# Two-layer trunk on one core: start addresses of the matmul operands in SBUF, modulo 256 bytes

## The chip, the cores and the metric

The kernel runs on one core of one Trainium2 chip. A core has a matrix engine (PE; its weight loads are listed apart as PEld), a vector engine (DVE), a scalar engine (ACT), a general engine (POOL) and a queue engine that issues DMAs (SP). SBUF is the on-chip memory that feeds the engines: 128 partitions, each a line of bytes; a tile takes the same byte range in every partition. PSUM receives the matmuls' results. The metric is the device time of one execution in microseconds; faster, same and slower are called at 2%.

## The reference

The input is x of shape (1, 256, 2048) in float32. Two layers follow, each a mixer and a squared-ReLU feed-forward, with RMS norms around both:

```python
for layer in range(2):
    y = rmsnorm(h, norm_w[layer, 0])
    if layer % 2 == 0:
        y = linear_attention_mixer(y, ...)   # gated DeltaNet heads | retention heads, one projection in, one out
    else:
        y = spatial_gating_mixer(y, ...)     # gelu(h @ w_in) -> u, v;  (u * (tril(W_s) layernorm(v) + b)) @ w_out
    h = h + rmsnorm(y, norm_w[layer, 1])
    y = squared_relu_mlp(rmsnorm(h, norm_w[layer, 2]), ffn_w_up[layer], ffn_w_down[layer])
    h = h + rmsnorm(y, norm_w[layer, 3])
```

`squared_relu_mlp` is `square(relu(h @ w_up)) @ w_down` with w_up (2048, 8192) and w_down (8192, 2048). The weights are read once each from HBM, some 475 MB in all, so the kernel is a stream of weights against 256 rows of activations.

## The kernel before

**Products in three matmuls.** A float32 product is made of matmuls in a reduced type. Each operand is split in a high part and a low remainder, and three matmuls per product are summed in PSUM: high x high, low x high, high x low. For weights, `weights` (lines 121 to 133) takes a block of 128 x 2048, loads it into `raw`, lets ACT write `whi` (line 131) and DVE write `wlo` (line 132). Activations are split the same way by `split` (lines 193 to 199).

**Which operand moves.** A matmul holds one operand of 128 x 128 in the array (it is loaded first, by a weight load, PEld) and streams the other, the moving one, past it. There are three kinds of loops:
- `prod_tok` (lines 135 to 140), called by `chunk_tok`, `first_chunk` and `down_last`: the activations, 128 rows of tokens, are held, and the weights move, up to 512 columns. It does all large products of the mixers, and in the feed-forward the first chunk of the up projection, column block 3 and half of column block 1 of the down projection, and its last block of rows.
- `up_pass` (lines 313 to 328): the weights are held, 128 columns of them, and the activations move, 256 tokens. It makes chunks 1 to 15 of the up projection.
- `chunk7` (lines 355 to 389): seven products instead of eight of a 2 x 2 block product, from sums of activations (`f`) and sums of weights (`qsum`); activations are held, 256 columns of weights move. It makes the rest of the down projection.

While one matmul runs, the next one's operand is loaded. The order in which blocks follow each other is written out in the feed-forward (`ORDER`, `FIRST`), and in the mixers small tasks are put between blocks by a counter (`spawn`, `tick`).

**Where tiles lie.** Pools of tiles are laid one behind the other from byte 1152 of a partition (below that are a scratch area and constants), and within a pool tiles lie in the order in which they are first asked for. The order of the pools is `gap`, `wp`, `cp`, `xp`, `hp`, and above them the pool of the stage at work: `l0`, `ffn1`, `sg`, `ffn3`.
- `gap` holds one unused tile of `PAD0` = 896 bytes (line 110), so `wp` begins at 2048. `wp` has 3 `raw`, 4 `whi` and 4 `wlo` of 8192 bytes, all at 0 modulo 256.
- `cp` holds small tiles, with an unused one of `PAD1` = 544 bytes in front (line 111), so that `xp` begins at 97280, again 0.
- `xp` holds the normed activations, `xh0` to `xh3` and `xl0` to `xl3` of 4096 bytes: all at 0. `new_x` makes them three times over: in layer 0's mixer (line 498) and in `down_last` (line 258) for the stage that follows.
- `hp` and the stage pools begin at 0 too. In the feed-forward, `e0`, `e1` (activations of the down projection) and `f0`, `f1` (their sums), each a pair of high and low tiles of 4096 bytes made by `pair` (line 387), lie at 0. In `sg`, two small tiles of 192 bytes come first, so that `v0` to `v7` lie at 128 and, after four more small ones, `u` and `e0` to `e3` at 0.
- `sg` uses its tiles twice: the gated activations that `sg_out` multiplies lie by turns in `e0` to `e3` (at 0) and in `v0` to `v7` (at 128). In layer 0 the held operand of the output projection lies in tiles of `hp` and `l0`, at 0 but for `Um0` and `Um1`, at 224.

Slices keep the place: a block of 512 weight columns is 2048 bytes, one of 256 is 1024, 128 tokens are 512 bytes. Only the first projection differs: it takes 400 columns of a block at a time, 1600 bytes, so that its four slices lie at 0, 64, 128 and 192.

Of the kernel before, what the change touches and what calls it, by code (L numbers as in the profile page):

```python
# [10 lines left out]
F32 = mybir.dt.float32  # L11
F32R = mybir.dt.float32r
# [5 lines left out]
P = 128  # L18
D = 2048
SEQ = 256  # L20
# [9 lines left out]
PARTS = [4, 2, 1, 1]  # L30
WAIT = [26, 30]
AHEAD = 200
PAD0, PAD1 = 896, 544
WARM = 10
SEVEN, KEPT = (0, 1, 2), 1
ORDER = (None, 0, None, 1, None, 2, None, 3)
# [59 lines left out]
def program(tc, nc, A, S):  # L96
# [3 lines left out]
    xp = tc.alloc_tile_pool(name="xp", bufs=1)  # L100
# [5 lines left out]
    V, G, ACT, PE, DMA = nc.vector, nc.gpsimd, nc.scalar, nc.tensor, nc.sync  # L106
    uid = [0]
    ahead = [0]

    V.memset(gap.tile([P, PAD0 // 4], F32, tag="gap0", name="gap0"), 0.0)  # L110
    V.memset(cp.tile([P, PAD1 // 4], F32, tag="gap1", name="gap1"), 0.0)

    def T(pool, shape, tag, dt=F32, bufs=None):
        uid[0] += 1
        kw = {} if bufs is None else {"bufs": bufs}
        return pool.tile(shape, dt, tag=tag, name=f"{tag}_{uid[0]}", **kw)
# [81 lines left out]
            ACT.activation(hi, src, AF.Copy, scale=col)  # L198
            V.scalar_tensor_tensor(lo, src, col, hi.bitcast(F32), ALU.mult, ALU.subtract)

    def group(pool, th, tl, bufs=None):
        return T(pool, [P, 4, SEQ], th, F32R, bufs), T(pool, [P, 4, SEQ], tl, F32R, bufs)

    def kts(groups):
        return [(e[0][:, j, :], e[1][:, j, :]) for e in groups for j in range(4)]

    def new_x(n=4):
        return [group(xp, f"xh{g}", f"xl{g}") for g in range(n)]

    def to_channels(src, dst, b, col=None):  # L210
        tp = bank(tpp, 512, "tp")
# [28 lines left out]
    h = [[None] * 4 for _ in range(2)]  # L240
# [14 lines left out]

    def down_last(s, X, rows, w1, w0, yw, rpend):
        units = [weights(s, [(r, [(c * 512, 512)]) for r in rows]) for c in range(4)]
        newx = None if w0 is None else new_x()
        rh = [None, None]
        rv = [None, None]  # L260
        for b in range(2):
            ssy = small(4, "ssy")
            yb = yw(b)
            for c in range(4):
                ps = bank(acc, 512, "acc")
                for j in range(4):
                    prod_tok(ps, X[j], b, units[c], j, 512, j == 0, j == 3)
                yt = y[b][c]
                V.tensor_tensor(yt, ps, yt, ALU.add)  # L269
                square_sum(ssy[:, c : c + 1], yt)  # L270
                (V if c == 3 else G).tensor_tensor(yb[c], yt, w1[c], ALU.mult)  # L271
                if c == 2:
                    base = small(1, "base")
                    V.tensor_reduce(base, ssy[:, 0:3], AX.X, ALU.add)
                    V.tensor_scalar(base, base, 1.0 / D, EPS if rpend is None else rpend[b], ALU.mult, ALU.add)
            rs = small(1, "rs")
            V.tensor_scalar(rs, ssy[:, 3:4], 1.0 / D, base, ALU.mult, ALU.add)
            rsqrt(rs, rs)
            for c in range(4):
                ht = h[b][c]  # L280
                V.scalar_tensor_tensor(ht, yb[c], rs, ht, ALU.mult, ALU.add)  # L281
                if w0 is None:
                    DMA.dma_start(A["out"][b * P : (b + 1) * P, c * 512 : (c + 1) * 512], ht)
                else:
                    (V if c == 0 else G).tensor_tensor(yb[c], ht, w0[c], ALU.mult)
                    to_channels(yb[c], newx[c], b)
        if w0 is not None:
            for b in range(2):
                ssh = small(4, "ssh")
                for c in range(4):  # L290
                    square_sum(ssh[:, c : c + 1], h[b][c])
                rh[b] = T(cp, [P, 1], f"rh{b}", bufs=2)
                tot = small(1, "tot")
                V.tensor_reduce(tot, ssh, AX.X, ALU.add)
                var = small(1, "var")
                V.tensor_scalar(var, tot, 1.0 / D, EPS, ALU.mult, ALU.add)
                rsqrt(rh[b], var)
                rv[b] = T(cp, [P, 1], f"rv{b}", bufs=2)
                V.tensor_scalar(rv[b], var, var, EPS, ALU.mult, ALU.mult)
            newx = kts(newx)  # L300
        return newx, rh, rv
# [81 lines left out]
    def ffn(up, dn, X, rh, w1i, w0i):  # L383
        last = HID // 512 - 1
        with tc.tile_pool(name=f"ffn{w1i}", bufs=1, reuse_waits="tile") as fp:

            def pair(name):
                return T(fp, [P, 4, SEQ], f"{name}h", F32R), T(fp, [P, 4, SEQ], f"{name}l", F32R)

            def relu2(ps):  # L390
                r = T(fp, [P, 512], "rl", bufs=3)
# [65 lines left out]
            t = []  # L457
# [36 lines left out]
    def layer0_mixer():  # L494
        rstd = [T(cp, [P, 1], f"rh{b}", bufs=2) for b in range(2)]
        s = S["la_in"]
        with tc.tile_pool(name="l0", bufs=1, reuse_waits="tile") as lp:
            xg = new_x()
            X = kts(xg)
            spans0 = [(4096, 16), (3072, 384)]  # L500
            ps = [bank(acc, 400, "acc") for _ in range(2)]
# [512 lines left out]
    def layer1_mixer(X, rh):  # L1014
        si, so = S["sg_in"], S["sg_out"]
        with tc.tile_pool(name="sg", bufs=1, reuse_waits="tile") as gp:
            ws = T(gp, [P, 8, P], "ws")
            DMA.dma_start(ws, A["ws"].rearrange("p (g t) -> p g t", t=P))
            G.affine_select(ws, ws, pattern=[[0, 8], [1, P]], compare_op=ALU.is_ge, fill=0.0, base=0,
                            channel_multiplier=-1)  # L1020
            v = [None] * 8
            st = [T(gp, [P, 8, 6], f"st{b}") for b in range(2)]

            def v_evac(c, b, ps):
                if v[c] is None:
                    v[c] = T(gp, [P, 2, 512], f"v{c}")
                ACT.activation(v[c][:, b, :], ps, AF.Gelu_apprx_tanh, scale=rh[b])
                V.bn_stats(st[b][:, c, :], v[c][:, b, :])

            for b, ps in first_chunk(si, X, [(SGW, 512)]):  # L1030
                v_evac(0, b, ps)
            for c in range(1, 8):
                ps = chunk_tok(si, X, ALLK, [(SGW + c * 512, 512)], 512)
                for b in range(2):
                    v_evac(c, b, ps[b])
            rs, mu = [], []
            for b in range(2):
                mv = T(gp, [P, 2], f"mv{b}")
                V.bn_aggr(mv, st[b])
                var = small(1, "var")  # L1040
                V.tensor_scalar(var, mv[:, 1:2], EPS, None, ALU.add)
                r = T(gp, [P, 1], f"lr{b}")
                rsqrt(r, var)
                rs.append(r)
                mu.append(mv[:, 0:1])

            tags = ["e0", "e1", "e2", "e3", "v0", "v1", "v2", "v3", "e0", "e1", "e2", "e3", "v4", "v5", "v6", "v7"]
            gts = [None] * 8

            def gate(g):  # L1050
                wb = T(hp, [P, 512], "bc", bufs=4)
                DMA.dma_start(wb, A["lnw"][:, g * 512 : (g + 1) * 512].partition_broadcast(P))
                bb = T(hp, [P, 512], "bc", bufs=4)
                DMA.dma_start(bb, A["lnb"][:, g * 512 : (g + 1) * 512].partition_broadcast(P))
                pss = []
                for b in range(2):
                    t = v[g][:, b, :]
                    V.tensor_scalar(t, t, mu[b], rs[b], ALU.subtract, ALU.mult)
                    G.tensor_tensor(t, t, wb, ALU.mult)
                    G.tensor_tensor(t, t, bb, ALU.add)  # L1060
                ps = chunk_tok(si, X, ALLK, [(g * 512, 512)], 512)
                us = []
                for b in range(2):
                    pm = bank(mxp, 512, "mx")
                    PE.matmul(pm, ws[:, g, :], v[g][:, b, :], start=True, stop=True)  # L1065
                    u = T(gp, [P, 512], "u", bufs=2)
                    ACT.activation(u, ps[b], AF.Gelu_apprx_tanh, scale=rh[b])
                    V.scalar_tensor_tensor(u, pm, bsc[:, g : g + 1], u, ALU.add, ALU.mult)
                    us.append(u)
                dst = (T(gp, [P, 4, SEQ], tags[2 * g], F32R), T(gp, [P, 4, SEQ], tags[2 * g + 1], F32R))  # L1070
                for b in range(2):
                    blocks_split(T(hp, [P, 512], "bc", bufs=4), us[b], dst, b)
                gts[g] = kts([dst])

            def rows(g):
                return [g * 512 + j * P for j in range(4)]

            gate(0)
            for a in (0, 2, 4):
                gate(a + 1)  # L1080
                gate(a + 2)
                down(so, gts[a] + gts[a + 1], rows(a) + rows(a + 1), a == 0)
            gate(7)
            down(so, gts[6], rows(6), False)

            def rows_in(tags):
                t = [T(gp, [P, 2, 512], g) for g in tags]
                return [t[0][:, 0], t[0][:, 1], t[1][:, 0], t[1][:, 1]]

            w1 = row_load(rows_in(["v0", "v1"]), "nrow", 2)  # L1090
            w0 = row_load(rows_in(["v2", "v3"]), "nrow", 6)
            return down_last(so, gts[7], rows(7), w1, w0, lambda b: rows_in(["e0", "e1"]), None)
# [62 lines left out]
```

## Time and profile before

| | us |
|---|---|
| median of 2 runs | 2518.86 (2517.79 to 2519.94) |
| profiled execution | 2520.84, span of its instructions 2519.1 |
| layer 0, mixer | from 0 to about 540 |
| layer 0, feed-forward | about 540 to 1255 |
| layer 1, mixer | about 1255 to 1803 |
| layer 1, feed-forward | about 1803 to 2519 |

The profile names an instruction by engine, source line and tiles, out<-in with buffer numbers left out; in a matmul's name the moving operand stands first, the held one second (`acc<-whi,xh`: weights move past activations; `tp<-xh,whi`: activations move past weights). A group's row has its count, the busy time and mean duration of one, and the idle time before it. Matmuls overlap in the pipeline and their ends are modelled, so the share of busy time of PE says that it always had a matmul under way, not how fast they followed each other; that is read from the distance of two starts. A row of the windows view has the window, its length, then the busy time and number of instructions of each engine, the granted clock of PE, the share of the DMA engines and GB/s.

### The profile page before, as it was taken

To read this page: it belongs to the slowest core of one execution; us is meant where nothing else is said; L and a number is where in the kernel's file an instruction comes from. 1 tells how busy PE (TensorE), PEld (TensorE's weight loads), DVE (VectorE), ACT (ScalarE), POOL (GpSimd) and SP (SyncE) were. 2 spreads that over 40 slices of the span, in tenths; PEclk is the share of its full clock that TensorE was granted. 3 is DMA by queue.
4 is the path that set the end of the run, shared out by engine and by line. 5 is a ranking of instruction groups with operands and counts; after the bars stand their busy time and mean duration, and the time that the engine had idled before them with its cause. 6 is when DMAs were issued, how large, how long until landed. Compare 5 with 4: busy or idle time off the path is not lost.

```text
span 2519.1 us, 37114 instructions
## 1 busy us (share of the span) xinstructions
PE 2485.1 (99%) x15418; PEld 2234.5 (89%) x15418; DVE 1984.7 (79%) x2322; ACT 1260.5 (50%) x1266; POOL 183.2 (7%) x144
## 2 busy tenths in 40 slices
PE   9999999999999999999999999999999999999998
PEld 8788888879999999999878878888799999999997
DVE  6586855578898889889864596876888988988897
ACT  6655444455455545455554434333555545555553
POOL 0001201130000000000210110110300000000001
PEclk9999999999999999999999999999999999999999
DMA  8444544644554555555455455555445555555553
GB/s 310 164 154 152 191 157 175 213 159 184 204 190 180 197 200 193 192 202 203 182 218 188 181 208 209 196 197 200 151 185 202 189 194 201 201 184 184 201 203 132
DMA packets 81832, 480.17 MB, mean 191 GB/s; under 512 B 13696, under 2 KB 15872, under 8 KB 27392
## 3 DMA queue, kind: packets, MB, share of 16 engines
q1 hardware_dynamic: 81664, 477.80, 52.5%
q8 instruction: 121, 1.98, 0.3%
q14 instruction: 47, 0.39, 0.0%
HBM read 475.14 MB, written 2.62 MB: 190 GB/s over the span
## 4 chain that ended last, share of the span: by engine, by line
PE 46%; DVE 3%; POOL 1%; issue 0%; ACT 0%; DVEq 0%; POOLq 0%; ACTq 0%
PE acc L138 8%; PE acc L140 8%; PE acc L139 8%; PE tp L326 5%; PE tp L325 5%; PE tp L324 5%; PE acc L368 1%; PE acc L370 1%; PE acc L369 1%; PE mx L370 1%; PE mx L369 1%; PE mx L368 1%; DVE h L281 1%; DVE wlo L132 1%; PE mx L1065 1%
## 5 line engine op out<-in xcount | busy, mean ns | idle before, releaser
L132 DVE TENSOR_TENSOR wlo<-raw,whi 128x2048 fp32r<-128x2048 f32 (+3 forms) x366 | 824.8, 2256 | 264.4 <-ACT whi L131 254.9
L131 ACT ACTIVATE whi<-raw 128x2048 fp32r<-128x2048 f32 (+3 forms) x366 | 686.4, 1876 | 469.9 <-PE acc L139 286.8
L326 PE MATMUL tp<-xh,wlo 128*128 128x256 f32 x1920 | 543.5, 283 | 0.0
L325 PE MATMUL tp<-xl,whi 128*128 128x256 f32 x1920 | 543.3, 283 | 0.0
L324 PE MATMUL tp<-xh,whi 128*128 128x256 f32 x1920 | 543.1, 283 | 0.0
L138 PE MATMUL acc<-whi,xh 128*128 128x512 f32 (+3 forms) x1120 | 439.3, 392 | 3.2 <-ACT whi L131 3.2
L140 PE MATMUL acc<-wlo,xh 128*128 128x512 f32 (+3 forms) x1120 | 431.5, 386 | 1.8 <-DVE wlo L132 0.9
L139 PE MATMUL acc<-whi,xl 128*128 128x512 f32 (+3 forms) x1120 | 431.8, 385 | 0.0
L324 PEld LDWEIGHTS tp<-xh,whi 128*128 128x128 f32 x1920 | 368.4, 192 | 1.7
L325 PEld LDWEIGHTS tp<-xl,whi 128*128 128x128 f32 x1920 | 368.4, 192 | 1.7
L326 PEld LDWEIGHTS tp<-xh,wlo 128*128 128x128 f32 x1920 | 368.4, 192 | 0.0
L138 PEld LDWEIGHTS acc<-whi,xh 128*128 128x128 f32 x1120 | 211.2, 189 | 43.5 <-ACT whi L131 4.4
L140 PEld LDWEIGHTS acc<-wlo,xh 128*128 128x128 f32 x1120 | 210.7, 188 | 42.9 <-DVE wlo L132 2.9
L195 ACT ACTIVATE whi<-qsum 128x2048 fp32r<-128x2048 f32 x74 | 141.7, 1915 | 210.4 <-DVE qsum L349 166.7
L139 PEld LDWEIGHTS acc<-whi,xl 128*128 128x128 f32 x1120 | 211.3, 189 | 38.7 <-issue 1.0
L196 DVE TENSOR_TENSOR wlo<-qsum,whi 128x2048 fp32r<-128x2048 f32 x74 | 169.4, 2290 | 66.1 <-ACT whi L195 66.1
L195 ACT ACTIVATE whi<-raw 128x1536 fp32r<-128x1536 f32 x74 | 110.2, 1489 | 184.5 <-DMA raw<-dn 70.2
L431 DVE TENSOR_TENSOR y<-acc,y 128x512 f32<-128x512 f32 x136 | 92.3, 686 | 56.0 <-PE acc L370 54.8
L196 DVE TENSOR_TENSOR wlo<-raw,whi 128x1536 fp32r<-128x1536 f32 x74 | 129.6, 1751 | 2.4 <-ACT whi L195 2.3
L271 POOL TENSOR_TENSOR e0h<-y,f1h 128x512 f32<-128x512 f32 x8 | 13.0, 1648 | 1364.8 <-DVE y L269 1364.8
L138 PE MATMUL acc<-whi,e0h 128*128 128x512 f32 x256 | 100.0, 391 | 0.0
L139 PE MATMUL acc<-whi,e0l 128*128 128x512 f32 x256 | 100.0, 391 | 0.0
(357 smaller groups left out, 4347.6 us busy)
## 6 DMA issues: line engine op xcount, KB each, us to landing
raw<-up SPq DMA_DIRECT2D x128, 1024.0 KB, 4.8
raw<-dn SPq DMA_DIRECT2D x128, 1024.0 KB, 4.8
raw<-sg_in SPq DMA_DIRECT2D x64, 1024.0 KB, 4.8
raw<-la_in SPq DMA_DIRECT2D x56, 1024.0 KB, 4.8
raw<-sg_out SPq DMA_DIRECT2D x32, 1024.0 KB, 4.8
raw<-la_out SPq DMA_DIRECT2D x16, 1024.0 KB, 4.7
raw<-la_in SPq DMA_DIRECT2D x4, 768.0 KB, 8.2
kq<-xT SPq DMA_DIRECT2D x8, 256.0 KB, 6.3
```

The costliest lines, as they stand in the source:

```text
L131: ACT.activation(a, r, AF.Copy)
L132: V.tensor_tensor(d, r, a.bitcast(F32), ALU.subtract)
L138: PE.matmul(ps, xh, wh, start=first, stop=False)
L139: PE.matmul(ps, xl, wh, start=False, stop=False)
L140: PE.matmul(ps, xh, wl, start=False, stop=last)
L195: ACT.activation(hi, src, AF.Copy)
L196: V.tensor_tensor(lo, src, hi.bitcast(F32), ALU.subtract)
L324: PE.matmul(out, wh[:, col], xh, start=k == 0 and m % 2 == 0, stop=False, skip_group_check=True)
L325: PE.matmul(out, wh[:, col], xl, start=False, stop=False, skip_group_check=True)
L326: PE.matmul(out, wl[:, col], xh, start=False, stop=k == NKT - 1, skip_group_check=True)
L368: PE.matmul(ps, x[k][0], wh, start=k == 0, stop=False, skip_group_check=True)
L431: V.tensor_tensor(Y[k, c], p, Y[k, c], ALU.add)
```

## The change

The paddings become 192 and 224 bytes. `wp` then begins at 1152 + 192 = 1344, which is 64 modulo 256: all weights, split or not, lie at 64. `cp` shifts with it, and `xp` begins at 96256, again 0, so `hp` and the stage pools still begin at 0.

The tiles of `xp` are made larger, 4160 and 4288 bytes, and hold the activations at an offset: `X_IN` = (64, 0) or `X_UP` = (0, 192), bytes within the high and the low tile. A low tile begins at 64 modulo 256, so `X_IN` puts both parts at 64 and `X_UP` both at 0. `down_last` takes `X_UP` where a mixer ends (there `rpend` is `None` and a feed-forward follows) and `X_IN` where a feed-forward ends.

`skip` makes an unused tile and writes zeros into it on POOL. In the feed-forward, 128 bytes of it stand before and behind each pair of `e0`, `f0`, `e1`, `f1` when it is first asked for: the pairs lie at 128, the other tiles of that pool at 0 as before. In `sg`, 192 bytes behind the two first small tiles put `v0` to `v7` at 64, and 128 bytes later put `u` and `e0` to `e3` at 64.

| operands of a matmul (held, moving), bytes modulo 256 | before | after |
|---|---|---|
| up projection, chunks 1 to 15 (weights, activations) | 0, 0 | 64, 0 |
| up projection, first chunk (activations, weights) | 0, 0 | 0, 64 |
| down projection (e or f, weights) | 0, 0 | 128, 64 |
| layer 0 input, layer 1 input (activations, weights) | 0, 0 | 64, 64 |
| layer 1 output, from e (activations, weights) | 0, 0 | 64, 64 |
| layer 1 output, from v (activations, weights) | 128, 0 | 64, 64 |
| layer 0 output (activations, weights) | 0 (Um 224), 0 | 0 (Um 224), 64 |

No instruction is taken away and none is moved; 18 memsets are added, and the two gap memsets become shorter.

```diff
-PAD0, PAD1 = 896, 544
+PAD0, PAD1 = 192, 224
+X_IN, X_UP = (64, 0), (0, 192)
...
+    def skip(pool, n):
+        uid[0] += 1
+        G.memset(pool.tile([P, n // 4], F32, tag=f"skip{uid[0]}", name=f"skip{uid[0]}"), 0.0)
...
-    def group(pool, th, tl, bufs=None):
-        return T(pool, [P, 4, SEQ], th, F32R, bufs), T(pool, [P, 4, SEQ], tl, F32R, bufs)
+    def group(g, at):
+        t = T(xp, [P, 1040], f"xh{g}", F32R), T(xp, [P, 1072], f"xl{g}", F32R)
+        return [a[:, o // 4 : o // 4 + 1024].rearrange("p (j t) -> p j t", t=SEQ) for a, o in zip(t, at)]
...
-    def new_x(n=4):
-        return [group(xp, f"xh{g}", f"xl{g}") for g in range(n)]
+    def new_x(at):
+        return [group(g, at) for g in range(4)]
...
-        newx = None if w0 is None else new_x()
+        newx = None if w0 is None else new_x(X_UP if rpend is None else X_IN)
...
             def pair(name):
-                return T(fp, [P, 4, SEQ], f"{name}h", F32R), T(fp, [P, 4, SEQ], f"{name}l", F32R)
+                if name in seen:
+                    return T(fp, [P, 4, SEQ], f"{name}h", F32R), T(fp, [P, 4, SEQ], f"{name}l", F32R)
+                seen.add(name)
+                skip(fp, 128)
+                hi = T(fp, [P, 4, SEQ], f"{name}h", F32R)
+                lo = T(fp, [P, 4, SEQ], f"{name}l", F32R)
+                skip(fp, 128)
+                return hi, lo
+
+            seen = set()
...
-            xg = new_x()
+            xg = new_x(X_IN)
...
             st = [T(gp, [P, 8, 6], f"st{b}") for b in range(2)]
+            skip(gp, 192)
...
+            skip(gp, 128)
             tags = ["e0", "e1", "e2", "e3", "v0", "v1", "v2", "v3", "e0", "e1", "e2", "e3", "v4", "v5", "v6", "v7"]
```

## The prediction

> **What bounds the kernel now.** I read the page's busy shares first, then the same by slice, then who waited for whom on PE, then the two feed-forward stretches alone.
>
> ```profile
> span 2519.1 us, 37114 instructions
> ...
> PE 2485.1 (99%) x15418; PEld 2234.5 (89%) x15418; DVE 1984.7 (79%) x2322; ACT 1260.5 (50%) x1266; POOL 183.2 (7%) x144
> ...
> PE   9999999999999999999999999999999999999998
> ...
> PEclk9999999999999999999999999999999999999999
> ```
>
> ```profile
> PE mx L697 <- DVE PT L700: 4.2, 3, 2.3
> ```
>
> ```profile
> 600.00:1235.00 635.00, 632.73 (x4762) 609.69 (x4761) 559.73 (x550) 333.47 (x255) 0.00 (x0) 1.00 0.54 194
> 1850.00:2510.00 660.00, 659.47 (x4938) 634.05 (x4937) 580.78 (x578) 343.70 (x272) 7.90 (x7) 1.00 0.52 189
> ```
>
> The matrix engine is busy in every slice, its granted clock is full, and its longest wait (4.2 us in all) is small. The two windows (length, then PE, PEld, DVE, ACT, POOL) lie within the two feed-forward layers: PE has no gap, DVE is at 559.73/635 = 88%. So the time is the pace at which matmuls follow each other, and a change of places pays or costs only through that pace. It must be read from start to start, because a matmul's end is modelled:
>
> ```profile
> 763.66 0.39 PE L140 MATMUL acc<-wlo,e0h 128*128 128x512 f32 x1
> ...
> 764.57 0.28 PE L324 MATMUL tp<-xh,whi 128*128 128x256 f32 x1
> 764.68 0.28 PE L325 MATMUL tp<-xl,whi 128*128 128x256 f32 x1
> 764.80 0.28 PE L326 MATMUL tp<-xh,wlo 128*128 128x256 f32 x1
> ...
> 765.88 0.28 PE L326 MATMUL tp<-xh,wlo 128*128 128x256 f32 x1
> ```
>
> Four 512-column matmuls take 764.57 - 763.66 = 0.91 us, 227 ns each; nine 256-column ones take 765.88 - 764.80 = 1.08 us, 120 ns each. The recorded durations keep a fixed distance to the pace (283 and 120, 391 and 227: about 163 ns), so a difference of durations in a grouped view is a difference of pace. The groups by form, with their counts:
>
> ```profile
> L326 PE MATMUL tp<-xh,wlo 128*128 128x256 f32 x1920 | 543.5, 283 | 0.0
> L325 PE MATMUL tp<-xl,whi 128*128 128x256 f32 x1920 | 543.3, 283 | 0.0
> L324 PE MATMUL tp<-xh,whi 128*128 128x256 f32 x1920 | 543.1, 283 | 0.0
> ...
> L138 PE MATMUL acc<-whi,e0h 128*128 128x512 f32 x256 | 100.0, 391 | 0.0
> ...
> L140 PE MATMUL acc<-wlo,v 128*128 128x512 f32 x128 | 50.6, 395 | 0.0
> L139 PE MATMUL acc<-whi,v 128*128 128x512 f32 x128 | 50.6, 395 | 0.0
> ...
> L140 PE MATMUL acc<-wlo,e 128*128 128x512 f32 x128 | 49.8, 389 | 0.0
> L139 PE MATMUL acc<-whi,e 128*128 128x512 f32 x128 | 49.8, 389 | 0.0
> ...
> L368 PE MATMUL acc<-whi,e1h 128*128 128x256 f32 x168 | 47.5, 283 | 0.0
> ...
> L370 PE MATMUL mx<-wlo,e0h 128*128 128x256 f32 x64 | 18.1, 283 | 0.0
> ```
>
> Lines 324 to 326 are 5760 matmuls; the groups of the seven-product blocks (lines 368 to 370, first and last shown) have 3108 more. These 8868 at 120 ns are 1064 us, 42% of the span, all in the feed-forward. It also has 1488 of 512 columns by the code (96 in the first chunk, 192 kept, 360 of column 3, 96 last, per layer).
>
> **What a place does, as this trace shows it.** The e and v rows are one stage, one loop and one weight stream, with idle time beside neither. By the layout the e tiles lie at 0 (mod 256) and the v tiles at 128, weights at 0: 128 bytes between moving and stationary operand cost 395 - 389 = 6 ns. So places matter, by several ns a matmul. The second place is the first projection: its weights are 400 columns wide, 1600 bytes, so its four slices lie at 0, 64, 128, 192 against activations at 0.
>
> ```profile
> 21.08 0.34 PE L138 MATMUL acc<-whi,xh 128*128 128x400 f32 x1
> ...
> 22.18 0.34 PE L138 MATMUL acc<-whi,xh 128*128 128x400 f32 x1
> ...
> 23.26 0.34 PE L138 MATMUL acc<-whi,xh 128*128 128x400 f32 x1
> ...
> 24.35 0.34 PE L138 MATMUL acc<-whi,xh 128*128 128x400 f32 x1
> ```
>
> From 21.08 six matmuls run with the moving operand at 192: 1.10/6 = 183.3 ns. From 22.18 six at 0: 1.08/6 = 180.0. From 23.26 six at 64: 1.09/6 = 181.7. What the change sets in both halves of the feed-forward is stationary minus moving = +64 (up: weights 64, activations 0; down: e and f 128, weights 64); moving 192 against stationary 0 is that same distance, and costs 3.3 ns over 0. I take it for the 512-column matmuls.
>
> For 256 columns the trace has no other distance, but it has other paces at the same one:
>
> ```profile
> L324 PEld LDWEIGHTS tp<-xh,whi x1920: 187/192/192, 566.1 to 2482.1; 128*128 128x128 f32 x192
> L324 PE MATMUL tp<-xh,whi x1920: 277/283/283, 566.4 to 2482.3; 128*128 128x256 f32 x192
> ```
>
> ```profile
> 214.78 0.28 PE L139 MATMUL acc<-whi,xl 128*128 128x256 f32 x1
> ...
> 215.60 0.28 PE L140 MATMUL acc<-wlo,xh 128*128 128x256 f32 x1
> ...
> 215.72 0.28 PE L138 MATMUL acc<-whi,xh 128*128 128x256 f32 x1
> ...
> 216.44 0.28 PE L138 MATMUL acc<-whi,xh 128*128 128x256 f32 x1
> ```
>
> Minimum 277, median and maximum 283: after a 512-column matmul the first one takes 764.68 - 764.57 = 0.11 us, and two later the pace is 120 and stays. In the mixer, after a gap, seven matmuls take 215.60 - 214.78 = 0.82 us, 117 ns each; then six take 0.72 us, 120 each. So 120 is a pattern into which loads and matmuls settle (load 192, not 187), and it is slower than what comes before it. [...]
>
> **The change part by part.**
> - 256-column matmuls, distance 0 to +64. Lower end: weight loads follow each other at 109 ns where the other stream is lighter (four transposes below, each with its own load: (600 - 272)/3 = 109), so 8868 x 11 = -97.5 us. Upper end: the 6 ns of the v rows, +53.2 us. I take 117, what the same shapes do before they settle: 8868 x 3 = -26.6 us.
>
> ```profile
> 214.22 0.60 PE L633 MATMUL tp<-ident,bc 128*128 128x128 f32 x4
> ```
>
> - 512-column matmuls of the feed-forward: 1488 x 3.3 = +4.9 us; ends 1488 x 6 = +-8.9 us (v against e; 277 against 283).
> - v tiles as stationary, distance 128 to 0: 384 x 6 = -2.3 us, at most that, at least 0.
> - Everything else in the mixers with weights and activations at 64: distance 0 as before, 0; the 3.3 ns of the projection rows on its 3,000-odd matmuls (+-10 us) bounds it if the place itself counts.
> - The output projection of layer 0: its operands stay at 0 while weights go to 64, distance -64: 336 x 1.7 = +0.6 us; ends 0 and +2.0.
> - 18 memsets of at most 192 bytes on POOL (16 in the feed-forward, 2 in layer 1), and shorter gap memsets on DVE.
>
> ```profile
> L504 POOL MEMSET Bn<- 128x128 f32 x1 | 0.2, 205 | 0.3 <-POOLq L1103 0.3
> ...
> L191 POOL TENSOR_TENSOR lr<-var,m 128x1 f32<-128x1 f32 x2 | 1.3, 668 | 164.0 <-DVE var L1041 164.0
> ```
>
> At most 0.2 us each, 3.6 us of POOL, which has 0.00 us of work in the first feed-forward window. The one in layer 1 may wait for the old tile under it; behind it in POOL's queue stands line 191, which idles 164 us before its input anyway. Without that cover it would be 0.4 us. I put 0.
> - Instructions, DMAs, data and queue order of ACT, DVE and SP are the same. A shorter feed-forward is covered as long as DVE keeps up: at 117 ns its share rises from 88% to about 90%; at 109 the first window shrinks by some 49 us and DVE's 559.73 us is 96% of it, so DVE's waits would be next.
>
> Sum: -26.6 + 4.9 - 2.3 + 0.6 = -23.4 us. The span of the profiled execution is 2519.1 us, its own time 2520.84, the median of the runs shown 2518.86; I take the sum from the median: 2495 us.
>
> [...]
>
> **The rivals.**
> - The 256-column pace falls to what the 277 ns row shows, 283 - 277 = 6 below 120, or one more: 8868 x 7 = -62.1, sum -58.9: 2460 us. For it: the row and the 0.11 at 764.57. Against: it is the first after a 512-column matmul, never a second.
> - It falls to 109: sum -94.3, 2424 us. For it: the transposes. Against: their moving stream is lighter, and DVE at 96% would hold part back.
> - The place does nothing: load and moving stream do not touch each other, 120 stays what it is, and time stays within 3 us of 2519. Against it: 395 against 389, 183.3 against 180.0. [...]
> - The 3.3 ns of distance +64 holds for 256 columns too: 8868 x 3.3 + 4.9 - 1.7 = +32: 2551 us.
> - Slower by the distance itself: distance 0 is the best that this trace shows at 512 columns (389 against 395), and the feed-forward leaves it. If every feed-forward matmul pays the 6 ns of the v rows: 10356 x 6 - 2 = +60: 2579 us. It decides from 5 ns a matmul on (50 us). For it: two of the three other distances seen are slower than 0 by 3 to 6 ns. Against: at 256 columns distance 0 is itself a settled slow pattern.
>
> **How the numbers follow.** 117 ns: 0.30, own range 2480 to 2512. 113 ns: 0.21. 109 ns: 0.17. Nothing: 0.10. 3.3 ns more: 0.06. 6 ns more: 0.16. Only the second and third pass 2%, which is about what a measurement of this kernel can tell from no change: faster 0.38; slower 0.16; within 0.46. The range leaves out the last case alone: 2422 (the 109 case with its 2 us of small terms) to 2556 (the 3.3 ns case with the 5 us of the 512-column end).
>
> **What would show it.** In the groups of lines 324 to 326 and 368 to 370, a mean of 280 (pace 117) and a load under 192 confirm the main step; 283 is the rival without effect; 276 or less the faster ones; 286 to 289 the slower ones. The feed-forward's 512-column rows (e0h, e0l) should read 394 to 395, the v rows 389 to 390, and the mixers' xh rows what they read now. Wrong would be a change in ACT or DVE durations, a new wait on PE, or time moving in the mixers, where I expect next to nothing.

## The result, and the profile after

| | before | after |
|---|---|---|
| median, us | 2518.86 (2517.79 to 2519.94) | 2489.39 (2488.07 to 2490.71) |
| profiled execution, us | 2520.84 | 2488.07 |
| span of its instructions, us | 2519.1 | 2486.3 |

The ratio is 0.988, with a 95% interval of 0.986 to 0.990: the kernel is about 29 us faster, which at 2% still counts as the same. The spans of the two profiled executions differ by 32.8 us, the medians by 29.5; the accounts below are of the profiled ones. First the page of after: the sum of each engine, then the costliest groups (busy time, mean ns of one, idle time before).

```profile
span 2486.3 us, 37131 instructions
...
PE 2453.0 (99%) x15418; PEld 2197.2 (88%) x15418; DVE 1977.6 (80%) x2322; ACT 1263.5 (51%) x1266; POOL 185.3 (7%) x162
...
L332 PE MATMUL tp<-xh,wlo 128*128 128x256 f32 x1920 | 535.2, 279 | 0.0
L330 PE MATMUL tp<-xh,whi 128*128 128x256 f32 x1920 | 535.2, 279 | 0.0
L331 PE MATMUL tp<-xl,whi 128*128 128x256 f32 x1920 | 535.0, 279 | 0.0
...
L331 PEld LDWEIGHTS tp<-xl,whi 128*128 128x128 f32 x1920 | 362.4, 189 | 1.9
```

Lines 330 to 332 are the former 324 to 326. Counts are unchanged but for the 18 memsets on POOL; PE is still at 99%. What moved is the mean of one matmul, 283 to 279, and with it the pace, which the prediction found some 163 ns below the recorded duration: 120 to 116. Lines 374 and 376 (once 368 and 370) and the 512-column rows, in the groups of after by form:

```profile
L143 PE MATMUL acc<-whi,e0h 128*128 128x512 f32 x256 | 101.2, 395 | 0.0
...
L145 PE MATMUL acc<-wlo,v 128*128 128x512 f32 x128 | 49.9, 390 | 0.0
L144 PE MATMUL acc<-whi,v 128*128 128x512 f32 x128 | 49.9, 390 | 0.0
...
L374 PE MATMUL acc<-whi,e1h 128*128 128x256 f32 x168 | 47.0, 280 | 0.0
...
L376 PE MATMUL mx<-wlo,e0h 128*128 128x256 f32 x64 | 17.8, 279 | 0.0
```

The feed-forward's 512 columns became slower (391 to 395) and the v rows faster (395 to 390). The time from each matmul's start to the next, summed by kind over the whole trace, waits included, gives the accounts (the last row has all matmuls, also those of kinds not listed, which change by +1.2 us together):

| kind of matmul | count | before, us (ns each) | after, us (ns each) | difference |
|---|---|---|---|---|
| up projection, 256 columns | 5760 | 691.6 (120.1) | 667.6 (115.9) | -24.0 |
| down projection, 256 columns | 3108 | 373.1 (120.1) | 361.2 (116.2) | -11.9 |
| 512 columns, e held (down) | 1295 | 301.0 (232.4) | 305.6 (236.0) | +4.6 |
| layer 1 output from v | 384 | 93.3 (243.0) | 91.6 (238.5) | -1.7 |
| 512 columns, normed activations held | 3072 | 721.2 (234.8) | 720.2 (234.4) | -1.0 |
| all | | 2509.6 | 2476.8 | -32.8 |

So the two 256-column stages give 35.9 us and the 512 columns of the down projection take 4.6 back. The 4.6 has two parts: 1277 steps without a wait became 5.3 ns longer each, +6.8 us, and the 18 others together 2.2 us shorter. A window of after inside the first feed-forward (columns as before) shows that nothing else has become the limit:

```profile
600.00:1227.00 627.00, 625.53 (x4796) 598.32 (x4795) 562.38 (x562) 338.34 (x264) 5.16 (x4) 1.00 0.55 200
```

DVE is at 562.38/627 = 90%, the granted clock is 1.00. The memsets on POOL, in the groups by line:

```profile
L116 POOL MEMSET skip<- 128x32 f32 (+1 forms) x18 | 1.4, 132 | 0.3 <-PE tp L219 0.3
```

**One mean, two paces.** The groups hide something that single starts show. One line in the view by source (minimum/median/maximum of the duration, first and last start), of after:

```profile
L330 PEld LDWEIGHTS tp<-xh,whi x1920: 187/188/192, 566.4 to 2448.9; 128*128 128x128 f32 x192
L330 PE MATMUL tp<-xh,whi x1920: 276/281/286, 566.6 to 2449.0; 128*128 128x256 f32 x192
```

The minimum is 276 and the median 281, while the mean is 279: a mixture. (The load's median is 188; it was 192.) The starts of successive stages, from the timeline of after (start, duration):

```profile
653.21 0.28 PE L330 MATMUL tp<-xh,whi 128*128 128x256 f32 x1
...
658.87 0.28 PE L374 MATMUL acc<-whi,e0h 128*128 128x256 f32 x1
...
663.64 0.28 PE L330 MATMUL tp<-xh,whi 128*128 128x256 f32 x1
...
669.30 0.40 PE L143 MATMUL acc<-whi,e0h 128*128 128x512 f32 x1
...
674.90 0.28 PE L330 MATMUL tp<-xh,whi 128*128 128x256 f32 x1
...
680.36 0.28 PE L374 MATMUL acc<-whi,e0h 128*128 128x256 f32 x1
```

These are stages of 48 up, 42 down, 48 up, 24 of 512 columns, and 48 up. Their paces: 5.66/48 = 118 ns, 4.77/42 = 114, 5.66/48 = 118, 5.60/24 = 233, 5.46/48 = 114. Same shapes, same distance, two paces, and each stage keeps its own from a few matmuls in to its end. Over the trace 61 of 118 long up stages run at 113.8 and 57 at 117.9; of the 72 down stages of 42 matmuls 27 at 113.6 and 45 at 117.7. Without the first few matmuls of a stage the paces are 113.3 and 117.8. Before, every one of them ran at 120.

That the period is 256 bytes and not 512 can be read off the layout. In each group of `xp` the high and the low tile now lie 256 bytes apart modulo 512, so lines 330 and 331, which hold the same `whi`, have distances of 64 and of 320 modulo 512. In the fast up stages the steps of both lines are 113.3 ns.

### The profile page after: what moved, and what is told of

It is laid out like the page before. It is cut to its first block, busy times and chain, and to the rows that moved or that the text cites. A ratio compares the mean times of both kernels' runs of the same rounds, so it can differ in the third digit from the quotient of the medians.

```text
span 2486.3 us, 37131 instructions
## 1 busy us (share of the span) xinstructions
PE 2453.0 (99%) x15418; PEld 2197.2 (88%) x15418; DVE 1977.6 (80%) x2322; ACT 1263.5 (51%) x1266; POOL 185.3 (7%) x162
## 4 chain that ended last, share of the span: by engine, by line
PE 46%; DVE 3%; POOL 1%; issue 0%; ACT 0%; DVEq 0%; POOLq 0%; ACTq 0%
PE acc L145 8%; PE acc L143 8%; PE acc L144 8%; PE tp L332 4%; PE tp L330 4%; PE tp L331 4%; PE acc L374 1%; PE acc L376 1%; PE acc L375 1%; PE mx L376 1%; PE mx L375 1%; PE mx L374 1%; DVE h L287 1%; DVE wlo L137 1%; PE mx L1082 1%
## 5 line engine op out<-in xcount | busy, mean ns | idle before, releaser
L332 PE MATMUL tp<-xh,wlo 128*128 128x256 f32 x1920 | 535.2, 279 | 0.0
L330 PE MATMUL tp<-xh,whi 128*128 128x256 f32 x1920 | 535.2, 279 | 0.0
L331 PE MATMUL tp<-xl,whi 128*128 128x256 f32 x1920 | 535.0, 279 | 0.0
L331 PEld LDWEIGHTS tp<-xl,whi 128*128 128x128 f32 x1920 | 362.4, 189 | 1.9
L330 PEld LDWEIGHTS tp<-xh,whi 128*128 128x128 f32 x1920 | 362.3, 189 | 2.0
L332 PEld LDWEIGHTS tp<-xh,wlo 128*128 128x128 f32 x1920 | 360.5, 188 | 0.0
L145 PE MATMUL acc<-wlo,e0h 128*128 128x512 f32 x256 | 101.2, 395 | 0.0
```

The source lines that it names most:

```text
L145: PE.matmul(ps, xh, wl, start=False, stop=last)
L330: PE.matmul(out, wh[:, col], xh, start=k == 0 and m % 2 == 0, stop=False, skip_group_check=True)
L331: PE.matmul(out, wh[:, col], xl, start=False, stop=False, skip_group_check=True)
L332: PE.matmul(out, wl[:, col], xh, start=False, stop=k == NKT - 1, skip_group_check=True)
```

## The experiments

A distance below is the place of the held operand minus that of the moving one, modulo 256 bytes, at 256 columns; before has 0 in up and down, the changed kernel +64 in both. Theory 1: only the distance counts. Theory 2, the rival: the absolute places do (weights away from 0, say). Differences in time are against before in the same comparison, whose medians there are 2519.76, 2519.58, 2519.23 and 2520.95 us. All diffs of the first eight are against the changed kernel.

### e1: undo the up half

The activations of the up projection go to 64, where its weights are: distance 0 at another place.

```diff
-X_IN, X_UP = (64, 0), (0, 192)
+X_IN, X_UP = (64, 0), (64, 0)
```

> Theory 1 (only the distance held minus moving counts, modulo 256): with the activations of the up projection at 64 like the weights, distance 0, its 5760 matmuls go back from 279 to 283 ns of recorded duration (120 ns from start to start); the down projection keeps 279 to 280. Time 2489 + 24 = about 2513 us (24 us is what these matmuls gained). Theory 2 (the places themselves count: weights and activations both off 0, away from the other tiles of the feed-forward): up stays at 279, time about 2489.

Measured: 2516.65 us, ratio 0.9985 (0.9976 to 0.9995). Groups by form of this run:

```profile
L330 PE MATMUL tp<-xh,whi 128*128 128x256 f32 x1920 | 543.6, 283 | 0.0
...
L374 PE MATMUL acc<-whi,e1h 128*128 128x256 f32 x168 | 47.3, 281 | 0.0
```

The up rows are back at 283 (from starts 119.9 ns) with all weights still at 64: the rival falls for this half. The miss is in the down half, which was not touched and yet rose from 116.2 to 117.8: with up at 120 ahead of them, none of the long down stages settles at 114 (72 of 72 run at 118).

### e2: undo the down half

The pairs e and f go to 64.

```diff
-                skip(fp, 128)
+                skip(fp, 64)
...
-                skip(fp, 128)
+                skip(fp, 192)
```

> Theory 1: with e and f at 64 like the weights, the 3108 matmuls of 256 columns in the down projection go back to 283 ns (+12 us), its 1296 of 512 columns back from 395 to 389-391 ns (-7 us); up keeps 279. Time about 2489 + 5 = 2494 us. Theory 2: 256 columns stay at 279 to 280, time about 2489 or less.

Measured: 2491.61 us, ratio 0.9882 (0.9865 to 0.9898). Groups by form, then starts of stages from the timeline, then the waits of PE (total, times, longest), all of this run:

```profile
L331 PE MATMUL tp<-xl,whi 128*128 128x256 f32 x1920 | 534.4, 278 | 0.0
...
L143 PE MATMUL acc<-whi,e0h 128*128 128x512 f32 x256 | 99.8, 390 | 0.0
...
L376 PE MATMUL mx<-wlo,e0h 128*128 128x256 f32 x64 | 18.1, 283 | 0.0
```

```profile
657.49 0.28 PE L374 MATMUL acc<-whi,e0h 128*128 128x256 f32 x1
...
662.52 0.29 PE L330 MATMUL tp<-xh,whi 128*128 128x256 f32 x1
...
667.99 0.39 PE L143 MATMUL acc<-whi,e0h 128*128 128x512 f32 x1
...
673.44 0.28 PE L330 MATMUL tp<-xh,whi 128*128 128x256 f32 x1
```

```profile
PE acc L143 <- DVE y L254: 6.6, 3, 4.5
```

The down rows return to 283 and their 512 columns to 390: distance 0 again, at 64. The stages from 657.49 on: down 5.03/42 = 120 ns, up 5.47/48 = 114, 512 columns 5.45/24 = 227. The up half, untouched, got better, 115.9 to 115.3: after a down stage at 120 most up stages take the fast pace (76 of the 118 long ones, against 61). The 4.5 us wait for `y` was 1.5 in the changed kernel (3.4 in all) and 2.3 in the kernel before (4.1 in all); I do not know what lengthened it.

### e3: keep the distances, shift all places

Weights, activations, e, f and the tiles of layer 1 all lie 64 bytes lower.

```diff
-PAD0, PAD1 = 192, 224
-X_IN, X_UP = (64, 0), (0, 192)
+PAD0, PAD1 = 128, 32
+X_IN, X_UP = (0, 64), (192, 0)
...
-        t = T(xp, [P, 1040], f"xh{g}", F32R), T(xp, [P, 1072], f"xl{g}", F32R)
+        t = T(xp, [P, 1072], f"xh{g}", F32R), T(xp, [P, 1040], f"xl{g}", F32R)
...
-                skip(fp, 128)
+                skip(fp, 64)
...
-                skip(fp, 128)
+                skip(fp, 192)
...
-            skip(gp, 192)
+            skip(gp, 128)
```

> All operands 64 bytes lower, every distance in the feed-forward and the mixers as in the changed kernel (weights 0, up activations 192, e and f 64, the rest 0; only the output projection of layer 0 returns to distance 0). Theory 1: rows as in the changed kernel (279 to 280 at 256 columns, 394 to 395 at 512 in the feed-forward), time 2488 us, one less for the output projection. Theory 2: with the weights back at 0 some of the gain goes: above 2500 us.

Measured: 2487.69 us, ratio 0.9868 (0.9853 to 0.9883). Groups by form of this run:

```profile
L332 PE MATMUL tp<-xh,wlo 128*128 128x256 f32 x1920 | 535.7, 279 | 0.0
...
L374 PE MATMUL acc<-whi,e1h 128*128 128x256 f32 x168 | 47.0, 280 | 0.0
```

Weights at 0 again, as before the change, and the gain is all there: 115.9 and 116.2 ns, even the split of the stages is the same (62 of 118 up stages fast, 28 of 72 down). Theory 2 falls.

### e4: the other sign

Distance -64 in both halves, made by the same lines (weights at 0, activations at 64 and e, f at 192).

> Distance -64 instead of +64 in up and down (weights 0, up activations 64, e and f 192). If it is enough to leave distance 0: 279 at 256 columns; and by the projection rows (1.7 ns against 3.3) the 512-column rows of the feed-forward fall to about 391: 2489 - 5 = about 2484 us. If the sign counts, 256 columns stay at 283 or go above: 2515 us or more.

Measured: 2501.39 us, ratio 0.9922 (0.9907 to 0.9937). Groups by form of this run:

```profile
L332 PE MATMUL tp<-xh,wlo 128*128 128x256 f32 x1920 | 537.2, 280 | 0.0
...
L374 PE MATMUL acc<-whi,e1h 128*128 128x256 f32 x168 | 46.9, 279 | 0.0
```

The sign matters. Both halves run at 117.8 ns, between the values I expected, and every long up stage runs at 117.7 to 117.9: a pace of 114 does not occur.

### e5 to e8: other distances

Four more, single runs beside one of before, made with the same paddings: up +32 with down +96, the reverse, 128 in both, and up -32 with down -96.

> Sweep of the distance (held minus moving) in the feed-forward, weights at 0: up +32, down +96. If what counts is in which 64-byte quarter of 256 bytes the two operands lie, +32 behaves in part like 0 and in part like +64 (279 to 283 ns, pace 118) and +96 in part like +64 and +128. If each distance has a pattern of its own, the two differ without order; a pace under 115 ns in either would be a better place than the change's. About 2490 to 2510 us.

> The same two distances with the parts exchanged: up +96, down +32. If the distance alone sets the pace, up has here the pace that the down projection had in the run before at 256 columns, and the other way round, within 1 ns. About 2490 to 2510 us.

> Distance 128 in up and down. The rows of v in the kernel before (distance 128) say 395 ns at 512 columns, like +64. At 256 columns between +64 (pace 116) and 0 (120): 118. About 2500 us.

> Up -32, down -96. -64 had a pace of 118 in both parts; -32 should lie between that and 0's 120, so 119, and -96 between -64 and 128. The tiles at 224 in layer 0's output (distance -32) read 394 to 395 ns at 512 columns. About 2505 us.

Measured: 2513.16, 2506.37, 2508.98 and 2505.86 us. All are slower than +64 and faster than 0. Here, for all distances tried, the mean pace of the long 256-column stages, and the mean step between 512-column matmuls of the down projection, worked out from the starts:

| distance | 256 columns, up / down, ns | 512 columns (down), ns |
|---|---|---|
| 0 | 120.0 / 120.0 | 227.9 |
| +32 | 118.3 / 118.3 | 233.1 |
| +48 (up), +80 (down) | 118.0 / 119.3 | |
| +56 (up), +72 (down) | 117.9 / 119.9 | |
| +64 | 113.8 or 117.9 / 113.6 or 117.7 | 233.2 |
| +96 | 118.2 / 117.6 | 234.2 |
| 128 | 118.6 / 118.7 | 232.3 |
| -64 | 117.8 / 117.8 | 229.4 |
| -32 (up), -96 (down) | 116.7 / 119.9 | 233.6 at -96 |

Three things follow. At 256 columns distance 0 is the worst, with +72 and -96 beside it, and at 512 it is the best of those tried. Where both halves were tried at one distance other than +64, their means agree within 0.6 ns, whatever the tiles. And a pace of 114 occurs at +64 only, though +96 mixes two paces as well: single stages settle at 117.3 (58 of 72 down, 46 of 118 up) or at 118.6 (the others). Two expectations missed: -32 is faster than every distance but +64, not at 119, and 128 took 9 us more than forecast. The +48 to +80 rows come from the two runs below; the run with up +32 and down +96 is the slowest of the four although its paces are no worse, because its 512-column matmuls cost more (310.5 us against 304 to 305) and have more waits (7.3 us against about 3).

### e9 to e11: a place for each use

If 256 columns want +64 and 512 want 0, weights should lie where their use wants them. This version starts from the kernel before, without the paddings, so that all other operands lie at 96 (or 224 in layer 1); each split weight tile is 256 bytes longer, `weights` takes the place as an argument, and a few small tiles of layer 1 share places in `cp` to make the room.

```diff
-PAD0, PAD1 = 896, 544
+D_UP, D_DOWN = 64, 64
+PLACE = 96
...
-    def weights(s, blocks, parts=1):
+    def wide(tag, bufs, at):
+        o = (at - 128) % 256 // 4
+        return T(wp, [P, 2112], tag, F32R, bufs=bufs)[:, o : o + 2048]
+
+    def weights(s, blocks, parts=1, at=PLACE):
...
-            wh, wl = weights(s, [(r, [(c * 512, 512)]) for r in ALLK[u * 4 : u * 4 + 4]])
+            wh, wl = weights(s, [(r, [(c * 512, 512)]) for r in ALLK[u * 4 : u * 4 + 4]], at=PLACE + D_UP)
...
-        hi = [T(wp, [P, 2048], "whi", F32R, bufs=HI_BUFS) for _ in range(2)]
-        lo = [T(wp, [P, 2048], "wlo", F32R, bufs=LO_BUFS) for _ in range(2)]
+        hi = [wide("whi", HI_BUFS, PLACE - D_DOWN) for _ in range(2)]
+        lo = [wide("wlo", LO_BUFS, PLACE - D_DOWN) for _ in range(2)]
```

Beside it, the same with `D_UP, D_DOWN` = 48, 80 and with 56, 72, to see how wide +64 is.

> Made from the kernel before, without padding tiles or skips: activations stay at one place and each block of split weights is put, within a tile 256 bytes longer, at the distance its own matmuls want: 0 for all of 512 columns (mixers, feed-forward, v and e alike), +64 for the 256 columns of up and of the seven-product blocks. If pace follows the distance alone: up and down at 256 columns 279 to 280 ns as in the changed kernel, the feed-forward's 512-column rows back at 389 to 391 (1296 x 5 ns = 6.5 us), the output projection of layer 0 back (1 us): 2489 - 7.5 = about 2482 us. If the 64-byte grid or the places themselves count (everything here lies at 32, 96, 160, 224): 2490 to 2520 us.

> The same kernel with distance +48 in up and +80 in the seven-product blocks. +32 and +96 had paces of 118.3 and 118. If +64 is the middle of a broad range, both read about 116 to 117; if it is a narrow place, both read 118. About 2482 to 2500 us.

> The same with +56 in up and +72 in the seven-product blocks, to see how near to +64 the pace of 116 holds. Broad: 116; narrow: 117 to 118. About 2482 to 2497 us.

Measured: 2487.11 us, ratio 0.987 (0.9852 to 0.9887); then 2507.65 and 2508.04, single runs. Eight bytes off +64 in both halves cost some 20 us: the pace of 114 occurs at +64 alone among the distances tried. (Behind a down stage at 120, where an up stage at +64 took 114 in e2, one at +56 took 118.) And the first of the three gained less than expected. Groups by form, one row by source, and the stages from the timeline, of the version with +64:

```profile
L327 PE MATMUL tp<-xh,wlo 128*128 128x256 f32 x1920 | 539.6, 281 | 0.0
...
L139 PE MATMUL acc<-whi,e0h 128*128 128x512 f32 x256 | 100.0, 391 | 0.0
...
L371 PE MATMUL mx<-wlo,e0h 128*128 128x256 f32 x64 | 17.7, 277 | 0.0
```

```profile
L369 PE MATMUL mx<-whi,f1h x168: 276/276/276, 617.4 to 2399.4; 128*128 128x256 f32 x168
```

```profile
652.83 0.28 PE L325 MATMUL tp<-xh,whi 128*128 128x256 f32 x1
...
658.48 0.29 PE L369 MATMUL acc<-whi,e0h 128*128 128x256 f32 x1
...
663.26 0.28 PE L325 MATMUL tp<-xh,whi 128*128 128x256 f32 x1
...
668.91 0.40 PE L139 MATMUL acc<-whi,e0h 128*128 128x512 f32 x1
```

The 512 columns are back at 391. But the mixture is another one: up 5.65/48 = 118 ns, down 4.78/42 = 114, up 5.65/48 = 118, and so through the trace (117 of 118 long up stages at 117.7, all 72 long down stages at 113.9). By the starts, up lost 678.7 - 667.6 = 11.1 us against the changed kernel, down gained 6.8 and the 512 columns 4.8: nothing is left. The median is 2 us below the changed kernel's, but the two ratios' intervals overlap for the most part.

### e12: distance or place, once more

Why does the same +64 give another mixture there? Either the 512-column stages between (distance 0 there, +64 in the changed kernel) leave the next stage in another state, or places modulo 64 count after all (32 there, 0 in the changed kernel). So all operands of that version were shifted by 32 bytes, distances kept (the diff is against that version); the two tiles `st0` and `st1` of layer 1 go to the place of `junk` in `cp` to make the room, and without them the operands of its output lie at the common place, so the weights there need no place of their own.

```diff
+    gap = tc.alloc_tile_pool(name="gap", bufs=1)
...
+    V.memset(gap.tile([P, 8], F32, tag="gap0", name="gap0"), 0.0)
...
-            st = [T(gp, [P, 8, 6], f"st{b}") for b in range(2)]
+            stt = T(cp, [P, 256], "junk", F32, bufs=1)
+            st = [stt[:, b * 48 : b * 48 + 48].rearrange("p (c s) -> p c s", s=6) for b in range(2)]
...
-                down(so, gts[a] + gts[a + 1], rows(a) + rows(a + 1), a == 0, PLACE + 128)
+                down(so, gts[a] + gts[a + 1], rows(a) + rows(a + 1), a == 0)
```

> The kernel with a place for every use, with every operand of a matmul 32 bytes higher and all distances kept (weights held at +64 over the activations at 256 columns, distance 0 at 512). In the run before it, each stage of 256-column matmuls at +64 settled on one of two paces and kept it to its end: the up stages at 118 ns (mean 117.8), the down stages at 114 (mean 114.0); in the changed kernel, same distance, both stages took both paces (115.9 and 116.2). Theory of distance and history: the places do not count, the difference comes from the 512-column stages between (distance 0 here, +64 there), so up 117.8, down 114.0 again and 2487 us. Rival, absolute places modulo 64 count (the operands lay at 32 modulo 64 there, at 0 modulo 64 in the changed kernel and in this run): up and down near 116 again, 5760 x 1.9 less and 3108 x 2.2 more, some 2483 us; the two paces decide, not the time.

Measured: 2487.29 us, ratio 0.9869 (0.9852 to 0.9885). Groups by form of this run:

```profile
L329 PE MATMUL tp<-xh,wlo 128*128 128x256 f32 x1920 | 539.4, 281 | 0.0
...
L373 PE MATMUL mx<-wlo,e0h 128*128 128x256 f32 x64 | 17.7, 277 | 0.0
```

Up 117.8, down 114.0, the same to 0.1 ns: the place does not count, modulo 64 either. What differs between this version and the changed kernel, besides places, is the distance of the 512-column stages. So what ran ahead of a stage at +64 seems to choose between its two paces. Counting, from the starts, the long stage just ahead of each long up stage at +64 in the traces of the changed kernel, of the down half undone (e2), of the place for each use (e9) and of this run (e12):

| ahead of the up stage | up stage at 114 | up stage at 118 |
|---|---|---|
| down at 120 (e2) | 72 | 0 |
| down at 118 (changed kernel) | 45 | 0 |
| down at 114 (changed kernel, e9, e12) | 0 | 27, 72, 72 |
| 512 columns at distance 0 (e2, e9, e12) | 0 | 42, 42, 42 |
| 512 columns at +64 (changed kernel) | 15 | 27 |

A slow down stage hands over a fast up stage and the other way round. The last row sorts itself out one stage further back: the up stage behind 512 columns at +64 took the pace that the up stage ahead of them did not have (118 behind 114, 27 of 27; 114 behind 118, 15 of 15; 28 of 28 and 14 of 14 in e3). Down stages behind an up stage at 114 took 118 (31 of 31 in the changed kernel). Behind one at 118 they took 114 where 512 columns had run ahead of that up stage (27 of 27) and 118 where a down stage had (14 of 14), but in e9 114 in both cases (72 of 72). The succession is regular in each of these traces, and the same one came back in e3; what carries it from stage to stage no run shows.

## Why the prediction was right, and where it was off

It said 2495 us (2422 to 2556), most likely within 2%; the time is 2489.39. By its own steps:

- **The place works through the pace, and nothing else changes: right.** No new wait: the longest of PE is 4.3 us in all (4.2 before), DVE's share came out at 90% as worked out for 117 ns, and the 18 memsets took 1.4 us together, and no one waited for them. That the distance between the two operands is what counts was taken for granted in the terms; shifting all places by 64 and by 32 bytes showed it (115.9 and 116.2 ns again by 64, 117.8 and 114.0 again by 32), and undoing one half at a time brought that half back to 120.
- **256 columns, "I take 117, what the same shapes do before they settle: 8868 x 3 = -26.6 us": mis-sized.** It measured -24.0 - 11.9 = -35.9 us, 116 ns. The step that failed is to expect one pace. At +64 there are two: about half of the up stages and a good third of the down stages (27 of 72) run at 114, the rest at 118. The row that I took for 117 and the 277 ns row that I gave to a rival ("the first after a 512-column matmul, never a second") are near to what became the two paces; at +64 the faster one holds for over 40 matmuls. That the mean landed beside 117 is chance: with other 512-column stages between, the same +64 gave 117.8 and 114.0.
- **512 columns, 1488 x 3.3 = +4.9 us: the sum came out by chance, its parts did not.** The 3.3 ns of the first projection, six steps that scatter from 182 to 184 ns against six from 178 to 186, was too small: +64 cost 5.3 ns a matmul in the down projection, +6.8 us, and waits that became 2.2 us shorter brought this to +4.6. And 192 of the 1488, the first chunks of the up projection, lie at -64 by the table of the change, not at +64; they cost about 1.6 ns each, which is the projection's figure for -64 (1.7). The rows read 395 as forecast, but there the duration grew by 4 ns and the pace by 5.
- **v tiles, -2.3 us: right**, -1.7; layer 0's output, +0.6: its matmuls take about 0.6 us more in sum; **mixers unchanged: right** within some 1 us of their 512 columns.
- **The rivals.** "The place does nothing" and the slower ones are out: 256 columns run at 120 ns at distance 0 and at 114 or 118 at +64, a half set back to distance 0 has a pace of 120 again, and with the up half set back (e1) the time is 3 us below that of before. The 109 ns case is out too: the fastest stages settle at 113.3.
- **The chances.** The range reached 73 us below the forecast and 61 above it, for an error of 6; its width came from not knowing which paces exist, and the trace of before, with one distance at 256 columns, could not tell.

What stays open: the runs show that the pace depends on the two places relative to each other (at 256 columns 120 ns at 0, 114 or 118 at +64, 117.8 at -64); by what means, no run shows. Why +64 has two paces, and how the pace of a stage comes to depend on the one before, is not settled beyond the successions above. A version that took 114 ns in every stage would by 5760 x (115.9 - 113.8) + 3108 x (116.2 - 113.6) gain another 20 us; but since a long down stage at 114 was always followed by an up stage at 118, +64 in both halves does not seem to give it; other ways were not tried.

## What to carry to other kernels

Where PE is at 99% and its waits are nothing, read the pace from start to start: a few ns a matmul, here 4 of 120, are 36 us, and in this kernel they depend on where the held and the moving operand lie to each other modulo 256 bytes (120 ns at 0, 116 on average at +64), not on where either lies (115.9 and 116.2 ns again with all places 64 bytes lower). Try a few distances for each shape by themselves, since what suits one shape (0 at 512 columns, 227.9 ns against 229.4 to 234.2) is among the worst for another (0 at 256, 120.0 against 113.6 to 119.9). And split a mean into stages before trusting it: 116 here is no pace that any stage has.

## What the runs showed of the hardware that was not expected

- Two settled paces at the same shapes and distance (113.8 and 117.9 ns at +64), each kept for a whole stage of 42 or 48 matmuls. Which one an up stage takes is regular: see the successions above. Two long stages at +64 in direct succession never both ran at 114 in these traces: behind a down stage at 114 the up stage ran at 118 (27 times in the changed kernel, 72 each in e9 and e12), behind an up stage at 114 the down stage did (31 times in the changed kernel).
- The effect is not symmetric: +64 has 114 and 118, -64 only 117.8. And it is narrow: +56 and +72 have 117.9 and 119.9.
- Changing the places of one half alone moved the pace of the other, once up and once down: 116.2 to 117.8 and 115.9 to 115.3.
